# Low parts of projection weights by an adding DMA, and attention's first keys projected inside GLA

## The chip, the cores and the metric

One core of a Trainium2 chip runs the kernel. The metric is device time in microseconds (us), the median of several executions. The core has five engines that run side by side, each in the order of its own instructions: TensorE (PE: matmuls; PEld is its weight load), VectorE (DVE), ScalarE (ACT), GpSimd (POOL) and SyncE (SP, which issues DMAs here). DMAs that SP issues go through one queue; those that POOL issues go through another, whose descriptors are made in software.

## The reference, cut to what matters

One encoder layer over 1024 tokens of width 1024, all in float32:

```python
n = rmsnorm(h, ln_g)
proj = n @ w_in                      # 1024 x 3104
qa, ka, va, qg, kg, vg, rg, zf, zb = split(proj)
y_na  = neighbourhood_attention(qa, ka, va, rpb)   # 8 heads x 64, on a 16 x 64 grid
y_gla = bidirectional_gla(qg, kg, vg, rg, zf, zb)  # 4 heads, chunks of 64
h = h + concat([y_na, y_gla]) @ w_out
h = h + square(relu(rmsnorm(h) @ w1)) @ w2
out = rmsnorm(h)
```

## The kernel before, in words

Everything is held with the features on the 128 partitions and the tokens along them. A float32 product is made of three passes of a shorter format (fp32r): each operand is split into a high part, which is the value rounded, and a low part, which is the rest, and `product` issues high by high, high by low and low by high.

The input projection is cut into 24 blocks of 128 columns: 0, 1 are GLA's queries and 2, 3 its keys (two heads each), 4 to 7 its values `v`, 8 to 11 its output gate `r`, 12 to 15 attention's queries, 16 to 19 its keys and 20 to 23 its values (two heads each, a "pair"). A block's weights are 128 x 1024 values, 512 KB. Blocks 0 and 2 are loaded and split at the start by other code (`load_w`). All the others go through `proj`, which calls `weights`: SP loads the block into `wf` (L165); `split` has ACT round it into `wh` (L173) and POOL subtract to give `wl` (L174). Each of the tiles `wf`, `wh` and `wl` has two buffers. Then, for each half of the tokens, 24 matmuls (eight steps of three) fill a PSUM bank, and an evacuation `ev` multiplies by the row norm `rms` and writes what the block is for.

The stages follow one another: norm of the input with the first projections; GLA, head by head; attention, pair by pair; the output projection; the MLP, which is over half of the time. PE executes its matmuls in the order in which the program issues them. The other engines' order comes from a scheduler, with a few priorities given by hand (`SOON_W` for weights).

In GLA and in attention the projections' steps serve as filler: `Fill` holds a list of generators, and `fill.run(n)` issues `n` steps of three matmuls each. `FILL_ORDER` is the order of the blocks in GLA, and `GLA_FILL[h]` says how many steps go at each of eleven places of head `h`:

- 0: after `gla_keys` (decayed keys and queries on DVE and ACT); 1: after `gla_ktok` (keys transposed, L116); 2 and 3: after the two halves of `gla_contrib` (`c`; its copies into `st` are ACT's), the latter with `gla_scan` (28 steps on DVE, L566 and L569);
- 4 and 5: after the halves of `gla_within` (scores `a` within chunks, masked into `asb` by DVE, L561); after 5 the gates of the next head (`gla_gates`: `la` on PE, then ACT, then DVE's scans into `b`, L490 and L492);
- 6 and 7: after `gla_intra`; 8 and 9: after `gla_inter`; 10: after the first half's norm (`gla_norm`: `ov` on PE, then ACT and DVE; it ends with the write to `yg`, L595).

GLA's blocks and attention's first queries have 176 steps; the table and the two runs ahead of it ask for 192, so that the list is empty from place 6 of the last head on.

After GLA, attention's first keys are projected without anything between their matmuls (`run(na_proj(0, "k", ...))`), then eight steps (`NA_PRE`) of its first values, then the scores of pair 0, block 0 (`softmax`, L752). `bias_for` loads the bias tile `bt` (L693) and finishes it on DVE with the mask `msk` (L698). The key tiles are three of 128 x 1024 for each of two alternating pairs, `k00`, `k10`, `k20` and `k01`, `k11`, `k21`: the high part of the first head, that of the second, and the low part of both. `na_proj`'s `ev` writes a high part twice by ACT (L393, L395) and a low part by DVE (L397; for queries POOL does it).

Memory is a stack from either end. GLA's tiles are in pools on the right (`gla0`, `gla`), attention's on the left (`na` with `msk` and `bt`, `qkv` with the keys); both use the same addresses, one after the other. A tile that uses an address again waits for the last user of the memory before it.

Of the kernel before, what the change touches and what calls it, by code (L numbers as in the profile page):

```python
# [10 lines left out]
F32 = mybir.dt.float32  # L11
F32R = mybir.dt.float32r
U32 = mybir.dt.uint32
AF = mybir.ActivationFunctionType
ALU = mybir.AluOpType
# [3 lines left out]
P = 128  # L19
D = 1024  # L20
T = 1024
H = 512
# [15 lines left out]
GLA_MID = 7  # L38
GLA_LATE = 8
GLA_FILL = (  # L40
# [4 lines left out]
)  # L45
FILL_ORDER = (('v', 0), ('r', 0), ('v', 1), ('q', 1), ('r', 1), ('v', 2), ('v', 3), ('r', 3), ('r', 2), ('n', 0))
SOON = 200
SOON_W = 100
SOON_O = 100
# [14 lines left out]
def block_kernel(ctx, tc, xT, g_mix, w_in, w_z, rpb, na_mask, gu, gb, g_gla, sel_f, sel_b,  # L64
                 rst, w_out, g_ff, w1, w2, g_fin, out):
    nc = tc.nc
    V, S, DMA, G = nc.vector, nc.scalar, nc.sync, nc.gpsimd

    L = "left"
    R = "right"  # L70
    pool = lambda name, side, bufs=1: tc.tile_pool(name=name, bufs=bufs, side=side)
# [7 lines left out]
    stg = stg_stack.enter_context(pool("stg", L, 2))  # L79
# [40 lines left out]
    class Fill:  # L120
# [24 lines left out]
        def run(self, steps=1 << 30):  # L145
            while steps > 0 and self.gens:
                steps -= self.step()
# [12 lines left out]

    def weights(block, eng=None):

        with tc.high_priority(offset=SOON_W):
            wf = stg.tile([P, D], F32, tag="wf", name="wf")
            DMA.dma_start(wf, block)  # L165
            return split(wf, eng)

    def split(wf, eng=None, steps=1):
        wh = stg.tile([P, D], F32R, tag="wh", name="wh")
        wl = stg.tile([P, D], F32R, tag="wl", name="wl")  # L170
        for i in range(steps):
            c = slice(i * D // steps, (i + 1) * D // steps)
            S.copy(wh[:, c], wf[:, c])  # L173
            (eng or V).tensor_tensor(wl[:, c], wf[:, c], wh[:, c].bitcast(F32), op=ALU.subtract)  # L174
        return wh, wl
# [50 lines left out]

    def proj(blk, evac):

        w = weights(w_in[blk], G)
        for hf in range(2):  # L230
            d = bank("mm", f"proj{blk}_{hf}")
            yield from proj_part(d, w, hf * H, H)
            evac(hf, d)

    fill = Fill()
    gla_stack = ExitStack()
    g0 = gla_stack.enter_context(pool("gla0", R))
    zT = g0.tile([P, T], F32R, tag="zT", name="zT")
# [5 lines left out]
    def qk_evac(g, which):  # L244

        dic, sc, t = ((qd, 0.125, "q"), (kd, 1.0, "k"))[which]
        for i in range(2):
            dic[2 * g + i] = g0.tile([P, T], F32, tag=f"{t}d{i}", name=f"{t}d{2*g+i}")

        def ev(hf, d):  # L250
            c = slice(hf * H, (hf + 1) * H)
            for i in range(2):
                dst = dic[2 * g + i]
                a, b = (slice(0, 64), slice(64, 128))[::1 - 2 * i]
                V.scalar_tensor_tensor(dst[a, c], d[a, :], sc, rms[a, c], op0=ALU.mult, op1=ALU.mult)  # L255
                S.copy(dst[b, c], dst[a, c])
        return ev
# [123 lines left out]
    def na_proj(p, nm, parts, tmp):  # L381

        def ev(hf, d):
            t = tmp()
            with tc.high_priority(offset=SOON):
                V.tensor_tensor(t, d, rms[:, hf * H:(hf + 1) * H], op=ALU.mult)
            x = [perm(x, hf) for x in parts]
            for i in range(2):  # L390
                own, other = slice(i * 64, i * 64 + 64), slice(64 - i * 64, 128 - i * 64)
                ti, hi = nat(t[own, :]), x[i][own]
                S.copy(hi, ti)  # L393
                if nm == "k":
                    S.copy(x[i][other], ti)  # L395
                lo, eng = (x[2][own], V) if nm == "k" else (x[i][other], G)
                eng.tensor_tensor(lo, ti, hi.bitcast(F32), op=ALU.subtract)  # L397
        return proj({"q": 12, "k": 16}[nm] + p, ev)
# [3 lines left out]
    q0 = [yn_p.tile([P, T], F32R, tag=f"yn{2 + i}", name=f"q0{i}") for i in range(2)]  # L402
# [16 lines left out]
                          rpb1[:, :, :, 15 - r:31 - r, :].rearrange("c h d a b -> c (h d) (a b)"))  # L419

    with pool("gla", R) as gp:
        vtok, keep = {}, {}
        gated, normed = set(), set()
        masks = []

# [176 lines left out]
        def first_q(_):  # L602
            return na_proj(0, "q", q0, lambda: gp.tile([P, H], F32, tag="g1", name="qt", bufs=2))

        def go(n):
            fill.run(n)

        for kind, i in FILL_ORDER:
            gen = {"v": gla_v, "r": gla_r, "q": gla_qk, "n": first_q}[kind](i)
            fill.add(gen, (kind, i))  # L610
        go(GLA_PRE)
        bs = {0: gla_gates(0, GLA_MID)}
# [72 lines left out]
    with pool("na", L) as ap, pool("qkv", L) as qp:  # L685
# [16 lines left out]
        def qk_tiles(p):  # L702

            f = lambda pl, tag: pl.tile([P, T], F32R, tag=tag, name=f"{tag}p{p}")
            q = q0 if p == 0 else [f(yn_p, "yn3"), f(qp, "qc")] if p == 2 else [f(qp, "qa"), f(qp, "qb")]
            return q, [f(qp, f"k{i}{p % 2}") for i in range(3)]

        def na_v(p):

            vT = []  # L710

            def transposes():
                vhl[p] = ap.tile([P, NB, 2, P], F32R, tag="vhl", name=f"vhl{p}")
                for g in range(2):
                    tb = bank("mm" if p + 1 == NH // 2 else "t", f"nvt{p}_{g}")
                    for i in range(4):
                        j = 4 * g + i
                        PE.transpose(tb[:, i * P:(i + 1) * P], vT[0][:, j * P:(j + 1) * P], ident)
                    src = tb.rearrange("p (a h d) -> p a h d", a=4, h=2)
                    hi = vhl[p][:, 4 * g:4 * g + 4, :, 0:64]  # L720
                    with tc.high_priority(offset=SOON_V):
                        S.copy(hi, src)
                        V.tensor_tensor(vhl[p][:, 4 * g:4 * g + 4, :, 64:128], src, hi.bitcast(F32),
                                        op=ALU.subtract)

            def ev(hf, d):

                if not hf:
                    vT.append(qp.tile([P, T], F32, tag=f"k2{1 - p % 2}", name=f"vT{p}"))
                with tc.high_priority(offset=SOON):  # L730
                    V.tensor_tensor(perm(vT[0], hf), nat(d), nat(rms[:, hf * H:(hf + 1) * H]), op=ALU.mult)
                if hf:
                    fill.later(NA_LATE, transposes, ("v", p))
            return proj(20 + p, ev)
# [81 lines left out]

        qt = lambda: qp.tile([P, H], F32, tag="qt", name="qt", bufs=2)
        qk = qk_tiles(0)
        run(na_proj(0, "k", qk[1], qt))
        fill.add(na_v(0), ("v", 0))  # L820
        bt = bias_for(0)
        fill.run(NA_PRE)
# [1 line left out]
        for p in range(NH // 2):  # L824
            if p > 1:
                yn.append(yn_p.tile([P, T], F32, tag=f"yn{p}", name=f"yn{p}"))
            if p + 1 < NH // 2:
                nxt = qk_tiles(p + 1)
                fill.add(na_proj(p + 1, "q", nxt[0], qt))
                fill.add(na_proj(p + 1, "k", nxt[1], qt), ("k", p + 1))  # L830
                fill.add(na_v(p + 1), ("v", p + 1))
            pt = [[ap.tile([P, 3, 3, P], F32R, tag=f"pt{i}{j}", name=f"pt{p}{i}{j}") for j in range(2)]
                  for i in range(2)]
            ob = {}
            for b in range(NB):
                fill.at(NA_FILL, p, b, 0)
                if b + 1 < NB:
                    xn = softmax(p, b + 1, *qk, bt)
                fill.at(NA_FILL, p, b, 1)
                turn(p, b, xs, pt)  # L840
                if b + 1 == NB and p + 1 < NH // 2:
                    fill.until(("k", p + 1))
                    qk, bt = nxt, bias_for(p + 1)
                    fill.run(NA_NEXT)
                    xn = softmax(p + 1, 0, *qk, bt)
                xs = xn
                fill.at(NA_FILL, p, b, 2)
                if b == 2:
                    fill.until(("v", p))
                    pv(p, 0, pt, ob)  # L850
                if b > 1:
                    pv(p, b - 1, pt, ob)
                if b == 2 and p + 1 == NH // 2:

                    n_stack.close()
                    hT = ctx.enter_context(pool("h", R)).tile([P, NK, T], F32, tag="hT", name="hT")
                    a1 = ctx.enter_context(pool("a1", R))
                    yhl[0] = half(a1, "y0")
                    DMA.dma_start(hT[:, :, 0:H], xT[:, :, 0:H])
                    to_parts(0, KO[:2], V)  # L860
                    for d in range(NK):
                        fill.add(sums(0, d, KO[:-1], G, ahead=KO[2:-1] if d == 0 else ()))
            pv(p, NB - 1, pt, ob)
# [621 lines left out]
```

## Time and profile before

| | |
|---|---|
| median of 3 runs | 1203.62 us (1203.04 to 1208.0) |
| profiled execution | 1203.34 us, its span 1201.6 us, mean granted TensorE clock 0.991 |
| PE, DVE, ACT, POOL busy | 1156.0, 896.8, 646.3, 282.6 us |
| PE matmuls | 5632 |
| POOL's subtractions `wl` (L174) | 36 (22 for `proj`'s blocks, 14 for `w_out`) |
| ACT's casts `wh` (L173) | 43 |

Times in rows of the timeline are microseconds from the start of the span. A row there reads: start, length, engine, line, operation, output<-inputs, shapes, count, and in brackets how long the engine had been idle before it and what ended that. The granted clock is 1.00 when TensorE's throttle lets all of it through.

### The profile page before, as it was taken

The page shows a single profiled execution, that of the slowest core. Times are in us where ns is not written, and L with a number is a line of the kernel's source. Part 1 is how long each engine was busy: PE and PEld are TensorE (multiplying, and loading weights), DVE is VectorE, ACT ScalarE, POOL GpSimd, SP SyncE. Part 2 cuts the span into 40 slices and gives each one's busy share as a digit, 9 for nine tenths or more (in the row PEclk, how much of TensorE's full clock was granted, in tenths as well). Part 3 has the DMA queues.
Part 4 walks back from the last instruction along what each step waited for, and adds up shares of the span by engine and source line. Part 5 has one row for each costly group of instructions (what it writes and reads, how often), then busy time and mean ns, then how long its engine had stood idle before and what let it go on. Part 6 is the DMA issues. An engine that isn't in the chain of part 4 may idle for free.

```text
span 1201.6 us, 15423 instructions
## 1 busy us (share of the span) xinstructions
PE 1156.0 (96%) x5632; PEld 946.8 (79%) x5632; DVE 896.8 (75%) x1558; ACT 646.3 (54%) x1201; POOL 282.6 (24%) x199
## 2 busy tenths in 40 slices
PE   9998999899999999999999999999999999999995
PEld 8877777687877878877778888888888888888775
DVE  8787778767868785695858885877859768597467
ACT  6766565545555665444643635546355463454654
POOL 5311101122131323530103230412304114041003
PEclk9999999999999999999999999999999999999998
DMA  7111010110111142230210122111211122111203
GB/s 236 50 58 52 25 36 19 35 57 19 49 36 49 32 156 92 104 123 1 70 59 26 58 70 69 35 55 53 71 53 35 53 70 70 53 36 53 71 1 140
DMA packets 37259, 73.02 MB, mean 61 GB/s; under 512 B 8928, under 2 KB 20320, under 8 KB 37184
## 3 DMA queue, kind: packets, MB, share of 16 engines
q1 hardware_dynamic: 36608, 71.11, 17.7%
q8 instruction: 44, 0.72, 0.2%
q0 software_dynamic: 432, 0.93, 0.2%
q14 instruction: 31, 0.25, 0.1%
q10 hardware_dynamic: 144, 0.00, 0.0%
HBM read 67.84 MB, written 5.96 MB: 61 GB/s over the span
## 4 chain that ended last, share of the span: by engine, by line
PE 70%; DVE 18%; ACT 8%; issue 2%; DMA 1%; SPq 0%; POOL 0%; DVEq 0%; ACTq 0%
PE f L111 24%; PE u L111 21%; PE proj L111 12%; PE op L111 5%; PE sc L111 2%; PE no L111 2%; PE pt L116 1%; DVE st L569 1%; DVE nl L284 1%; DVE b L492 1%; DVE b L490 1%; DVE st L566 1%; DVE pl L958 1%; DVE nf L888 1%; DVE fsq L1388 1%
## 5 line engine op out<-in xcount | busy, mean ns | idle before, releaser
L958 POOL TENSOR_TENSOR ul<-uB,uh 128x512 fp32r<-128x512 f32 x84 | 109.2, 1319 | 330.4 <-ACT uh L993 213.4
L980 ACT CAST ph<-A 128x512 fp32r<-128x512 f32 x166 | 103.0, 621 | 146.2 <-PE f L111 73.6
L174 POOL TENSOR_TENSOR wl<-wf,wh 128x1024 fp32r<-128x1024 f32 x36 | 88.8, 2467 | 333.8 <-ACT wh L173 310.6
L111 PE MATMUL f<-uh,ph 128*128 128x512 f32 x400 | 155.8, 390 | 1.5 <-ACT u L1001 1.4
L111 PE MATMUL f<-ul,ph 128*128 128x512 f32 x400 | 155.7, 389 | 0.1
L111 PE MATMUL f<-uh,pl 128*128 128x512 f32 x400 | 155.7, 389 | 0.0
L958 DVE TENSOR_TENSOR pl<-A,ph 128x512 fp32r<-128x512 f32 x166 | 112.8, 689 | 52.6 <-ACT ph L980 52.6
L111 PE MATMUL proj<-nh,wh 128*128 128x512 f32 x352 | 150.9, 429 | 0.8 <-DVE qd L255 0.8
L111 PE MATMUL proj<-nh,wl 128*128 128x512 f32 x352 | 139.6, 397 | 0.0
L111 PE MATMUL proj<-nl,wh 128*128 128x512 f32 x352 | 139.4, 396 | 0.0
L1140 DVE TENSOR_TENSOR hT<-hT,f 128x512 f32<-128x512 f32 x168 | 113.0, 687 | 19.9 <-PE f L111 19.9
L111 PE MATMUL u<-n,ph 128*128 128x512 f32 x288 | 89.2, 391 | 2.0 <-ACT ph L893 2.0
L111 PEld LDWEIGHTS f<-uh,ph 128*128 128x128 f32 x400 | 75.1, 188 | 17.9 <-ACT u L1001 1.8
L111 PEld LDWEIGHTS f<-ul,ph 128*128 128x128 f32 x400 | 75.1, 188 | 16.0 <-DVE ul L958 0.4
L111 PEld LDWEIGHTS f<-uh,pl 128*128 128x128 f32 x400 | 75.1, 188 | 15.6
L111 PEld LDWEIGHTS proj<-nh,wh 128*128 128x128 f32 x352 | 66.9, 190 | 19.8 <-issue 5.2
L993 ACT CAST uh<-uB 128x512 fp32r<-128x512 f32 x84 | 51.9, 618 | 51.3 <-PE f L111 34.5
L111 PE MATMUL u<-T,ph 128*128 128x512 f32 x256 | 79.2, 391 | 0.1
L111 PEld LDWEIGHTS proj<-nh,wl 128*128 128x128 f32 x352 | 67.1, 191 | 15.2
L111 PEld LDWEIGHTS proj<-nl,wh 128*128 128x128 f32 x352 | 67.4, 191 | 11.5 <-issue 1.4
L111 PE MATMUL op<-y,wh 128*128 128x512 f32 x240 | 75.8, 396 | 0.4 <-DVE y L665 0.4
L111 PE MATMUL u<-nt,ph 128*128 128x512 f32 x224 | 68.9, 389 | 0.0
(297 smaller groups left out, 2484.5 us busy)
## 6 DMA issues: line engine op xcount, KB each, us to landing
A<-in_w SPq DMA_DIRECT2D x64, 512.0 KB
wf<-in_w_in SPq DMA_DIRECT2D x22, 512.0 KB
wf<-in_w_out SPq DMA_DIRECT2D x17, 512.0 KB
hT<-in_xT SPq DMA_DIRECT2D x2, 2048.0 KB
xs<-in_xT SPq DMA_DIRECT2D x6, 512.0 KB
out<-hT SPq DMA_DIRECT2D x4, 512.0 KB
out<-hT SPq DMA_DIRECT2D x8, 256.0 KB
rpb<-rpb SPq DMA_DIRECT2D x16, 96.0 KB
```

The lines of the kernel that those rows point to most:

```text
L111: m = nc.tensor.matmul(*args, **kw)
L116: tc.keep_in_program_order(nc.tensor.transpose(*args, **kw))
L174: (eng or V).tensor_tensor(wl[:, c], wf[:, c], wh[:, c].bitcast(F32), op=ALU.subtract)
L284: V.scalar_tensor_tensor(nl[:, k, sl], xs[:, k, :], gmix[:, k:k + 1], nh[:, k, sl].bitcast(F32), op0=ALU.mult, op1=ALU.subtract)
L490: V.tensor_tensor_scan(b[0:64, c], rsts[0:64, :], m[0:64, :], 0.0, op0=ALU.mult, op1=ALU.add)
L492: V.tensor_tensor_scan(b[64:128, c][:, ::-1], rsts[64:128, ::-1], m[64:128, ::-1], 0.0, op0=ALU.mult, op1=ALU.add)
L566: V.scalar_tensor_tensor(st[0:64, i + 1, :], st[0:64, i, :], dec[0:64, i:i + 1], st[0:64, i + 1, :], op0=ALU.mult, op1=ALU.add)
L569: V.scalar_tensor_tensor(st[64:128, j - 1, :], st[64:128, j, :], dec[64:128, j:j + 1], st[64:128, j - 1, :], op0=ALU.mult, op1=ALU.add)
L958: return kp(eng.tensor_tensor(l, x, h.bitcast(F32), op=ALU.subtract))
L980: kp(S.copy(ph, x))
L993: kp(S.copy(uh, x))
L1140: kp(V.tensor_tensor(hT[:, d, c], hT[:, d, c], o[:, s], op=ALU.add))
```

## The change

`weights` has a second way to make a block's low part, used for all of `proj`'s blocks but block 4: ACT writes the negated rounded weights into `wl`, and a DMA issued by POOL adds the block, read again from HBM, to it; ACT then makes `wh` with a pass of its own. The output projection's weights keep `split`.

Attention's first keys become the last entry of `FILL_ORDER`, `("k", 0)`, and their projection ahead of attention is gone. The table asks for eight more steps: two at place 5 of head 0, one at place 5 of head 2, one at place 1 and four at place 3 of head 3. Counted through, that puts four of the 16 steps ahead of the last head's second `gla_contrib` (they push later blocks' steps forward) and twelve at its places 3 to 8. So that the tiles exist then, GLA's first and second query and key tiles and the key tiles `k00`, `k10`, `k20` share a new pool `glak`, which lies on the right under GLA's others and is closed late in attention.

```diff
-    (17, 4, 3, 3, 5, 3, 2, 3, 6, 0, 3),
+    (17, 4, 3, 3, 5, 5, 2, 3, 6, 0, 3),
     (8, 2, 5, 2, 4, 2, 3, 3, 5, 0, 4),
-    (10, 4, 3, 4, 4, 3, 4, 3, 6, 0, 2),
-    (13, 3, 3, 4, 3, 2, 3, 3, 3, 0, 7),
+    (10, 4, 3, 4, 4, 4, 4, 3, 6, 0, 2),
+    (13, 4, 3, 8, 3, 2, 3, 3, 3, 0, 7),
...
-FILL_ORDER = (..., ('r', 2), ('n', 0))
+FILL_ORDER = (..., ('r', 2), ('n', 0), ('k', 0))
...
             DMA.dma_start(wf, block)
-            return split(wf, eng)
+            if eng is not None:
+                return split(wf, eng)
+            wl = stg.tile([P, D], F32R, tag="wl", name="wl")
+            S.activation(wl, wf, AF.Copy, scale=-1.0)
+            G.dma_start(wl, block, accum_op=ALU.add)
+            wh = stg.tile([P, D], F32R, tag="wh", name="wh")
+            S.copy(wh, wf)
+            return wh, wl
...
-        w = weights(w_in[blk], G)
+        w = weights(w_in[blk], G if blk == 4 else None)
...
+    k_stack = ExitStack()
+    gk = k_stack.enter_context(pool("glak", R))
...
-            dic[2 * g + i] = g0.tile([P, T], F32, tag=f"{t}d{i}", name=f"{t}d{2*g+i}")
+            dic[2 * g + i] = (g0 if t == "q" and i else gk).tile([P, T], F32, tag={"k0": "k00", "q0": "k10", "k1": "k20"}.get(f"{t}{i}", "qd1"), name=f"{t}d{2*g+i}")
...
+        def first_k(_):
+
+            k0.extend(gk.tile([P, T], F32R, tag=f"k{i}0", name=f"k{i}0p0") for i in range(3))
+            yield from na_proj(0, "k", k0, lambda: gp.tile([P, H], F32, tag="g1", name="qt", bufs=2))
...
-            return q, [f(qp, f"k{i}{p % 2}") for i in range(3)]
+            return q, k0 if p == 0 else [f(qp if p % 2 else gk, f"k{i}{p % 2}") for i in range(3)]
...
-                    vT.append(qp.tile([P, T], F32, tag=f"k2{1 - p % 2}", name=f"vT{p}"))
+                    vT.append((gk if p % 2 else qp).tile([P, T], F32, tag=f"k2{1 - p % 2}", name=f"vT{p}"))
...
-        run(na_proj(0, "k", qk[1], qt))
...
+                    k_stack.close()
                     n_stack.close()
```

More of the change, by code (lines that the diff above doesn't have):

```diff
@@ L40 @@
 GLA_FILL = (
[1 row of a table removed]
[1 row of a table added]
     (8, 2, 5, 2, 4, 2, 3, 3, 5, 0, 4),
[2 rows of a table removed]
[2 rows of a table added]
 )
-FILL_ORDER = (('v', 0), ('r', 0), ('v', 1), ('q', 1), ('r', 1), ('v', 2), ('v', 3), ('r', 3), ('r', 2), ('n', 0))
+FILL_ORDER = (('v', 0), ('r', 0), ('v', 1), ('q', 1), ('r', 1), ('v', 2), ('v', 3), ('r', 3), ('r', 2), ('n', 0), ('k', 0))
 SOON = 200
@@ L421, in block_kernel @@
     with pool("gla", R) as gp:
-        vtok, keep = {}, {}
+        vtok, k0 = {}, []
         gated, normed = set(), set()
@@ L608, in block_kernel @@
         for kind, i in FILL_ORDER:
-            gen = {"v": gla_v, "r": gla_r, "q": gla_qk, "n": first_q}[kind](i)
+            gen = {"v": gla_v, "r": gla_r, "q": gla_qk, "n": first_q, "k": first_k}[kind](i)
             fill.add(gen, (kind, i))
```

## The prediction

> **What bounds the kernel now.** I read the busy shares first, then the busy time by stage, then the slow instructions of DVE beside POOL, then TensorE's waits. The page's head and its engine rows, with the row of the removed instruction:
>
> ```profile
> span 1201.6 us, 15423 instructions
> PE 1156.0 (96%) x5632; PEld 946.8 (79%) x5632; DVE 896.8 (75%) x1558; ACT 646.3 (54%) x1201; POOL 282.6 (24%) x199
> L174 POOL TENSOR_TENSOR wl<-wf,wh 128x1024 fp32r<-128x1024 f32 x36 | 88.8, 2467 | 333.8 <-ACT wh L173 310.6
> ```
>
> TensorE (PE) is busy for 96% and does the same matmuls after the change, so at most its idle time and its slow-clock time can be won. Busy time by stage says where these lie (columns: engine busy times with counts, then the granted clock, the DMA engines' share, GB/s):
>
> ```profile
> 60.00:252.00 192.00, 174.73 (x999) 139.44 (x998) 150.26 (x239) 109.40 (x176) 32.00 (x20) 0.96 0.12 38
> 252.00:440.00 188.00, 185.34 (x945) 147.98 (x944) 146.18 (x392) 113.27 (x276) 42.11 (x24) 1.00 0.12 40
> 120.00:140.00 20.00, 17.56 (x108) 13.32 (x107) 15.62 (x35) 8.61 (x14) 2.38 (x1) 0.91 0.13 37
> 180.00:200.00 20.00, 17.96 (x106) 14.80 (x102) 15.67 (x26) 7.31 (x12) 2.36 (x1) 0.91 0.07 27
> 235.00:246.00 11.00, 7.86 (x35) 6.08 (x34) 9.60 (x21) 0.62 (x1) 1.04 (x1) 0.69 0.00 0
> ```
>
> GLA (60 to 252) leaves PE idle for 192.0 - 174.7 = 17.3 us and loses clock after its waits: (1 - 0.91) x 20 = 1.8 us twice and (1 - 0.69) x 11 = 3.4 us near its end. Attention (252 to 440) leaves 2.7 us. All that this change can win is about 27 us.
>
> What makes PE wait in GLA is the DVE chain, and POOL's subtraction lengthens it. The timeline, POOL's row first, then DVE's:
>
> ```profile
> 56.32 2.76 POOL L174 TENSOR_TENSOR wl<-wf,wh 128x1024 fp32r<-128x1024 f32 x1 [2.91 <-ACT wh L173]
> 55.67 1.22 DVE L490 TENSOR_TENSOR_SCAN b<-rsts,lm 64x512 f32<-64x512 f32 x1
> 56.90 3.26 DVE L492 TENSOR_TENSOR_SCAN b<-rsts,lm 64x512 f32<-64x512 f32 x1
> 87.19 1.57 DVE L569 SCALAR_TENSOR_TENSOR st<-st,dec 64x128 f32<-64x128 f32 x1
> 89.51 2.67 DVE L569 SCALAR_TENSOR_TENSOR st<-st,dec 64x128 f32<-64x128 f32 x7
> 126.26 3.80 DVE L566 SCALAR_TENSOR_TENSOR st<-st,dec 64x128 f32<-64x128 f32 x7
> 147.59 3.43 DVE L490 TENSOR_TENSOR_SCAN b<-rsts,lm 64x512 f32<-64x512 f32 x1
> 183.45 2.21 DVE L569 SCALAR_TENSOR_TENSOR st<-st,dec 64x128 f32<-64x128 f32 x1
> ```
>
> The reader is to see one scan take 1.22 and the next 3.26 us, with POOL's subtraction beside it; a step of the state scan takes 2.67 / 7 = 0.38 us, but 1.57 or 2.21 when it is caught. The PE rows with a wait, and what ended it:
>
> ```profile
> 71.02 1.09 PE L116 MATMUL kt<-ident,kD 128*128 128x128 f32 x8 [1.43 <-DVE kD L508]
> 93.00 0.50 PE L111 MATMUL la<-zT,guh 128*128 128x512 f32 x1 [2.36 <-DVE asb L561]
> 134.29 0.48 PE L111 MATMUL a<-qD,kI 64*128 64x128 f32 x2 [0.94 <-DVE asb L561]
> 167.58 1.13 PE L116 MATMUL kt<-ident,kD 128*128 128x128 f32 x8 [0.70 <-ACT nu L205]
> 186.47 1.16 PE L111 MATMUL a<-qD,kI 64*128 64x128 f32 x14 [2.04 <-DVE asb L561]
> 239.66 0.80 PE L111 MATMUL a<-qD,kI 64*128 64x128 f32 x2 [2.80 <-DVE asb L561]
> 240.79 2.07 PE L111 MATMUL a<-qD,kI 64*128 64x128 f32 x14 [0.34 <-DVE asb L561]
> ```
>
> That the stalled instructions lie on the way to the end is shown by the chain that ended last, in which they stand (start, length, piece):
>
> ```profile
> 56.90 3.27 DVE b L492
> 87.19 1.57 DVE st L569
> ```
>
> **Part 1: low parts by an adding DMA.** 21 of the 22 weight blocks that `proj` loads (all but block 4) lose the POOL subtraction: 21 x 2.467 = 51.8 us less on POOL. Each gains a second 128x1024 pass on ACT and a DMA that POOL issues.
>
> Stalls won, each the smaller of DVE's excess and the PE wait behind it: 3.26 - 1.22 = 2.0 against 1.43, take 1.4; 1.57 - 0.38 = 1.2 at 93.00, of which the two fill steps added there leave 1.0; 3.80 - 2.67 = 1.1 against 0.94, take 0.9; 3.43 - 1.22 = 2.2 against 0.70, take 0.7; 2.21 - 0.38 = 1.8 against 2.04, take 1.8. Sum -5.8 us; ends 0 (another wait ends last) and -7.5 (the five waits whole). Two clock drops follow these waits (those of 120 to 140 and 180 to 200). I take both as gone, -3.6 us; ends 0 and -3.6.
>
> ACT's added passes, by rows of ACT and of PE:
>
> ```profile
> 221.06 1.03 ACT L173 CAST wh<-wf 128x1024 fp32r<-128x1024 f32 x1
> 224.19 1.16 PE L111 MATMUL c<-vtok,kt 64*128 64x128 f32 x16 [1.08 <-ACT kt L525]
> ```
>
> Some ten of the 21 fall in GLA. Where ACT then idles or DVE is the later one, 1.05 us more costs nothing. Here at 221.06 ACT already makes PE wait. I count two of ten on the path, +2.1 us; ends 0 and 10 x 1.05 = +10.5. ACT in attention is busy for 113 of 188 us and gets 11 x 1.05 = 11.6 more, while DVE loses its stalls. PE's projection steps cover both, and I take 0; ends -2.7 (the stage's whole idle time) and +3 (three passes caught).
>
> The adding DMA must land before the third matmul of a step of its block. Rows of the first and the last of the 21 blocks (`r` of head 0, `v` of attention's last pair): the cast, the first matmul with `wl`; and what DMAs from POOL's queue took for 256 KB (last column: issue to landing):
>
> ```profile
> 46.28 1.04 ACT L173 CAST wh<-wf 128x1024 fp32r<-128x1024 f32 x1
> 56.01 0.39 PE L111 MATMUL proj<-nh,wl 128*128 128x512 f32 x1
> 399.67 1.05 ACT L173 CAST wh<-wf 128x1024 fp32r<-128x1024 f32 x1
> 417.32 0.40 PE L111 MATMUL proj<-nh,wl 128*128 128x512 f32 x1
> rsts<-in_rst POOLq DMA_DIRECT2D x1, 256.0 KB, 8.5
> msk<-in_na_mask POOLq DMA_DIRECT2D x1, 256.0 KB, 3.4
> ```
>
> From the end of the pass to the use stand 56.0 - 47.3 = 8.7 us and 417.3 - 400.7 = 16.6 us; worked out alike, the others have 11.7, 12.5, 13.4, 14.2 and then 15.9 or more. No row has an adding DMA of 512 KB. Its bounds are 3.4 us (undisturbed, if bytes cost little) and 17 us (twice the queued 8.5). It is nearest to the undisturbed row, since the queue is otherwise empty: some 6 us, all hidden, 0; ends 0 and +29 us (17 us against each block's time). The second reading of 0.5 MB x 21 over 380 us adds 29 GB/s to 38, where the DMA engines are busy for 0.12: free. POOL waits for ACT as before; behind it stand `st`'s memsets and the low parts of the queries, which then come earlier. `wf` is freed by ACT, not POOL, so SP's loads are issued about 2.4 us sooner.
>
> The Trainium skill, "DMA: Bandwidth & Descriptors", section "Anatomy of one DMA", fits such a DMA as 2.0 us plus its bytes over 436 GB/s; with the two source reads that "Collectives: The Full Stack" counts for an add (section "The bandwidth ceiling"), an estimate is 4.4 us, and the term stays 0.
>
> **Part 2: first attention keys inside GLA.** Sixteen fill steps (48 matmuls) leave the place between GLA and attention: four go ahead of head 3's second contribution, twelve into its tail. Of the four, two lie in the wait at 93.00 (counted), one in that at 224.19, and one costs +0.7 us on the way. The rows of the seam (the first is the chain's, 24 steps without a break, 0.68 us each):
>
> ```profile
> 252.90 16.33 PE proj L111 x72
> 260.60 0.68 DVE L397 TENSOR_TENSOR k20p<-qt,k00p 64x512 fp32r<-64x512 f32 x1
> 262.63 0.69 DVE L595 TENSOR_TENSOR yg<-ny,o 128x512 f32<-128x512 f32 x1
> 263.52 0.38 SPq L693 DMA_DIRECT2D bt<-rpb  x1
> 265.21 2.48 DVE L397 TENSOR_TENSOR k20p<-qt,k00p 64x512 fp32r<-64x512 f32 x1 [0.69 <-ACT k00p L393]
> 269.11 1.82 DVE L698 SCALAR_TENSOR_TENSOR bt<-bt,msk 128x384 f32<-128x384 f32 x4
> 271.45 0.42 DVE L752 CUSTOM_DVE_ANT_0 xsc<-sc,bt 128x256 f32<-128x256 f32 x1
> ```
>
> Twelve steps in the tail are 8.2 us. They fill its wait (2.80 + 0.34 us) and its clock loss (3.4), 6.5 in all, so the norm starts 1.6 us later. But attention cannot start when PE is free: the bias `bt` is loaded into GLA's memory, right behind its last norm (`yg`, ended 263.3), and the first softmax waits for it. The change leaves this as it is. The norm and the bias are rid of key work on DVE: two halves of 0.7 us inside the norm, one between the bias's parts. So the first softmax moves by +1.6 - 1.4 - 0.7 = -0.5 us, though 10.9 us of PE work have left its way. PE, with eight steps of `v`, its scores and four steps more, is done some 8 us early and waits for `bt`: a new wait, which eats the filled one. Ends: +1.6 (DVE's relief doesn't reach) and -2.3 (the stalled 2.48, 1.8 over its neighbours' 0.68, counts whole as well). A wait of that length brings a clock drop; by the two 1.8 us rows, +1.8; ends 0 and +3.4.
>
> The keys' own evacuation (eight casts of ACT, six of DVE's 0.7 us) lies beside the tail's steps. Their `wf` load passes on SP ahead of `bt`, as before, and their adding DMA on POOL ahead of the mask's.
>
> **Sum.** -5.8 - 3.6 + 2.1 + 0 + 0 + 0.7 - 0.5 + 1.8 = -5.3 us. The profiled execution took 1203.3 us (span 1201.6), about the median of 1203.62. Forecast 1198.0 us.
>
> **The rivals.**
> Late adding DMAs (slower). For it: nothing here shows one, and POOL makes its descriptors while DVE is 78% busy (150.26 of 192). Against: the spare times. At 17 us each the blocks are late by 29 us together, 1227; it decides (slower by over 0.5%) from about 14.4 us on, where 11 us are lost. The Trainium skill, "SBUF — State Buffer", section "SBUF: two separate sides", has this rule: POOL is locked out of writing descriptors while DVE runs an instruction that takes both ports. If that held for all of DVE's busy time, 3.4 us would become 3.4 / 0.22 = 15.5 us and 17 us would be lost.
> ACT takes DVE's place: all ten passes on the path, 8.4 us over my two, 1206. For: 224.19. Against: ACT is busy for only 109 of 192 us.
> The stalls were not the limit, and the clock drops stay: +9.4, 1207. Against: the stalled rows in the chain.
> More is won: no ACT cost, no drop at the seam, attention's 2.7 us gone: 1191.4.
>
> **How the numbers follow.** About 0.5%, 6 us, is what can be told from no change; the border is 1197.6. Forecast case 0.50 (1194 to 1202): 0.31 faster, 0.19 same. More won 0.14, faster. ACT or no limit 0.23: 0.19 same, 0.04 slower. Late DMAs 0.13: 0.11 slower, 0.02 same. Faster 0.45, same 0.40, slower 0.15. The range, 1191 to 1206, leaves out the late DMAs and the ends of the others.
>
> **What would show it.** The scans all at 1.22 us and the state steps at 0.38; PE waits under 1 us at 71, 134 and 186 with the clock at 1.00 there; none at the second `a` of head 3; a wait of some 8 us ahead of the scores of block 1, ended by `bt`; `proj` with `wl` never waiting for a DMA. I am wrong if PE waits for `wl`, if ACT ends the waits that DVE ended, or if the seam's wait is far from 8 us.

## The result, and the profile after

The changed kernel takes 1218.8 us (median; 1218.1 to 1219.3) against 1203.5 us: 1.0118 of the time before, with an interval of 1.0094 to 1.0143. It is slower by some 15 us, where 1198 was forecast and 1191 to 1206 was the range.

The page of the changed kernel, as the lines shown of before, with the added DMA's issues:

```profile
span 1216.1 us, 15445 instructions
PE 1164.6 (96%) x5632; PEld 953.5 (78%) x5632; DVE 874.8 (72%) x1558; ACT 665.2 (55%) x1222; POOL 246.4 (20%) x199
wl<-in_w_in POOLq DMA_DIRECT2D x21, 512.0 KB, 7.8
```

DVE is busy for 22 us less, POOL for 36 less, ACT for 19 more. The adding DMA lands after 7.8 us (its last column; the forecast assumed 6, and the estimate of 4.4 beside it falls further short), and no wait of PE in this trace was ended by it. PE is busy for 8.6 us more with the same 5632 matmuls, which fits the stretches at half clock below. The waits of PE that are new or grew, or were forecast to go and stayed:

```profile
106.92 0.77 PE L111 MATMUL proj<-nh,wh 128*128 128x512 f32 x1 [4.99 <-DVE qd L265]
247.04 0.49 PE L111 MATMUL a<-qD,kI 64*128 64x128 f32 x2 [2.80 <-DVE asb L571]
266.38 1.90 PE L111 MATMUL ov<-osq,ones 128*128 128x512 f32 x2 [2.13 <-ACT osq L595]
284.59 0.69 PE L111 MATMUL sc<-k00p,q 128*128 128x384 f32 x1 [6.45 <-DVE sm L767]
```

The reader is to see that none of them names `wl`. The granted clock (the figure after POOL's, 0.5 where it is halved) drops behind the first three of them and, at the fourth, from within the wait; busy times in those windows:

```profile
106.40:116.60 10.20, 9.68 (x29) 7.72 (x30) 0.98 (x2) 3.57 (x7) 0.40 (x2) 0.51 0.63 153
249.80:253.20 3.40, 3.40 (x15) 2.94 (x13) 1.52 (x3) 0.39 (x1) 0.00 (x0) 0.54 0.00 0
266.80:270.20 3.40, 3.40 (x8) 2.02 (x7) 1.24 (x2) 2.55 (x5) 0.00 (x0) 0.53 0.73 143
280.50:290.70 10.20, 5.98 (x16) 4.21 (x17) 6.89 (x24) 3.26 (x10) 0.00 (x0) 0.51 0.12 45
```

The same PE instructions set side by side with before say where the time went. At head 0's first state products (`o<-qD,st`, at 100 us before) the changed kernel leads by 2.9 us; at head 0's first norm matmul (113) it is 5.2 late. At head 3's second contribution (233) it is 4.8 late, at its first norm matmul (263) 12.3, at the scores of block 2 (292) 15.0. From there to the end of the kernel it stays between 13 and 15. Two places lose all of it: 107 us, and the stretch from 233 us on, that is GLA's tail and the seam between GLA and attention.

Place one. DVE's rows and what the wait of 4.99 us was for (`qD` of head 1 reads `qd`, then the next heads' `qd` is written into the same memory):

```profile
104.84 1.21 DVE L524 TENSOR_TENSOR qD<-qD,qd 128x1024 f32<-128x1024 f32 x1
106.08 1.30 DVE L265 SCALAR_TENSOR_TENSOR qd<-proj,rms 64x512 f32<-64x512 f32 x2
```

`proj` has two PSUM banks. The 17th step of blocks 1 and 3 opens a third and needs the first back, whose evacuation writes `qd` where head 1's queries still lie. Before, that step stood at place 10 of head 0. The two steps added at place 5 move it to place 8, ahead of head 0's last state products, and PE, in order, stands in front of it.

Place two, from the last norm to the first softmax, on DVE, SP and POOL:

```profile
274.68 0.69 DVE L746 TENSOR_TENSOR vT<-proj,rms 128x512 f32<-128x512 f32 x1 [2.89 <-PE proj L111]
277.46 0.69 DVE L605 TENSOR_TENSOR yg<-ny,o 128x512 f32<-128x512 f32 x1
278.35 0.38 SPq L708 DMA_DIRECT2D bt<-rpb  x1
278.75 0.56 POOL L702 DMA_DIRECT2D msk<-in_na_mask  x1 [14.15 <-DVE yg L605]
282.30 1.90 DVE L713 SCALAR_TENSOR_TENSOR bt<-bt,msk 128x256 f32<-128x256 f32 x5 [4.15 <-DMA msk<-in_na_mask]
284.11 0.41 DVE L767 CUSTOM_DVE_ANT_0 xsc<-sc,bt 128x256 f32<-128x256 f32 x1
```

The last norm ends at 278.15, 14.8 us later than before; the bias load goes out 0.2 us behind it, the mask's 0.6 us. DVE's row names the mask as the one that landed last; both lie in memory that GLA used, and both wait for this norm.

### The profile page after: what moved, and what is told of

Its sections match the earlier page's. It is cut to its first block, busy times and chain, and to the rows that moved or that the text cites. A ratio compares the mean times of both kernels' runs of the same rounds, so it can differ in the third digit from the quotient of the medians.

```text
span 1216.1 us, 15445 instructions
## 1 busy us (share of the span) xinstructions
PE 1164.6 (96%) x5632; PEld 953.5 (78%) x5632; DVE 874.8 (72%) x1558; ACT 665.2 (55%) x1222; POOL 246.4 (20%) x199
## 4 chain that ended last, share of the span: by engine, by line
PE 76%; DVE 13%; ACT 6%; issue 2%; DMA 1%; SPq 0%; POOL 0%; DVEq 0%; ACTq 0%; POOLq 0%
PE f L111 24%; PE u L111 21%; PE proj L111 15%; PE op L111 5%; PE sc L111 2%; PE no L111 2%; DVE st L579 1%; PE pt L116 1%; PE o L111 1%; DVE pl L973 1%; DVE asb L571 1%; DVE nf L903 1%; PE sb L111 1%; PE ob L111 1%; DVE st L576 1%
## 5 line engine op out<-in xcount | busy, mean ns | idle before, releaser
L111 PE MATMUL proj<-nh,wh 128*128 128x512 f32 x352 | 153.8, 437 | 6.8 <-DVE qd L265 5.0
L111 PEld LDWEIGHTS proj<-nh,wh 128*128 128x128 f32 x352 | 68.2, 194 | 26.5 <-issue 5.9
L171 POOL DMA_DIRECT2D wl<-in_w_in x21 | 18.7, 891 | 266.7 <-ACT wl L170 248.6
```

What stands on the lines that cost most here:

```text
L111: m = nc.tensor.matmul(*args, **kw)
L171: G.dma_start(wl, block, accum_op=ALU.add)
```

## The experiments

Theory A: the adding DMA wins what was forecast, and the moved projection steps lose more. Theory B: the loss comes with the adding DMA (ACT's passes, late low parts). Behind each median stands its ratio to the kernel before, measured in the same group of runs, with a 95% interval; the kernel before had 1205.4, 1203.9, 1203.9 and 1205.2 us in the four groups, and 1203.5 in that of the result. A difference between medians of two groups, such as one to the changed kernel's 1218.8, is therefore good to about 2 us only.

**One part at a time.** The adding DMA alone:

```diff
 kernel before
+            if eng is not None: return split(wf, eng)
+            ... adding DMA as in the change
-        w = weights(w_in[blk], G)
+        w = weights(w_in[blk], G if blk == 4 else None)
```

> The kernel before with the adding DMA alone (21 blocks), attention's first keys where they were. Theory A (the loss is the moved projection steps: at 107 us PE stands 5 us in front of a full bank, and at the seam it waits for the bias): this is faster than before by 4 to 9 us, 1194 to 1200, with no wait over 2 us at 107 and none at the scores of block 1. Theory B (the loss comes with the adding DMA, by the added ACT passes or by low parts that land late): 1208 to 1218, with both waits in place.

Measured: 1195.3 us, 0.9915 (0.990 to 0.993). 10 us faster, theory A's range; B falls. At the second contribution of head 3 it leads by 8.9 us, and at the end of the two traces by 8.4.

The keys alone:

```diff
 changed kernel
-        w = weights(w_in[blk], G if blk == 4 else None)
+        w = weights(w_in[blk], G)
```

> The changed kernel with all low parts subtracted by POOL again; the keys inside GLA and the changed table stay. Theory A: 1213 to 1222, about as slow as the changed kernel or slower, with the wait at the scores of block 1 over 5 us. Theory B: 1200 to 1206.

Measured: 1231.9 us, 1.0215 (1.020 to 1.023): slower than even A allowed. Both waits are there (4.99 and 6.45 us), PE stands for another 5.38 us behind the gate's evacuation (`rm`), and the wait in front of head 3's second scores has doubled:

```profile
230.93 0.79 PE L111 MATMUL proj<-nh,wh 128*128 128x512 f32 x1 [5.38 <-DVE rm L460]
...
260.13 0.79 PE L111 MATMUL a<-qD,kI 64*128 64x128 f32 x2 [5.91 <-DVE asb L571]
```

So the parts are -10 and +26.5 us alone, +15 together.

**The first place.** Two steps moved from place 5 to place 10:

```diff
-    (17, 4, 3, 3, 5, 5, 2, 3, 6, 0, 3),
+    (17, 4, 3, 3, 5, 3, 2, 3, 6, 0, 5),
```

> The changed kernel with the two added steps of head 0 moved from place 5 to place 10, behind the last state products and the first norm. Theory A: the wait of 5 us at 107 and the clock drop of 10.2 us behind it go, 8 us are won there, some of it lost again later: 1209 to 1214. Theory B: 1217 to 1220, since the bank is late for another reason than the steps' place.

Measured: 1211.4 us, 1.0053 (1.0036 to 1.0070). The wait at that bank is back to what it was, and 7.4 us of the changed kernel's median are won (in the traces 8.0 us at head 3's second contribution, 6.1 at the last matmul):

```profile
107.59 0.47 PE L111 MATMUL proj<-nh,wh 128*128 128x512 f32 x1 [0.82 <-DVE qd L265]
```

The same entry put into the good kernel:

```diff
 adding DMA alone
-    (17, 4, 3, 3, 5, 3, 2, 3, 6, 0, 3),
+    (17, 4, 3, 3, 5, 5, 2, 3, 6, 0, 3),
```

> The adding DMA alone, with the one table entry of the change, two more steps at place 5 of head 0. Theory: these bring the third bank of the next projections ahead of head 0's last state products; PE stands 5 us at 107 and the clock drops behind it: 1200 to 1206. Rival (the wait needs the other entries too): 1194 to 1197.

Measured: 1209.3 us, 1.0037 (1.0021 to 1.0052). The one number costs 14 us here, more than expected: 7.6 us at the bank, and later another clock drop of 20.5 us (from 238 us on), where every later place has other steps; that these are the reason was not tested apart.

```profile
106.81 0.76 PE L111 MATMUL proj<-nh,wh 128*128 128x512 f32 x1 [4.99 <-DVE qd L262]
```

**The second place.** Pair 0's bias replaced (it is left out, and old values stand in its stead, so nothing is waited for):

```diff
-        bt = bias_for(0)
+        bt = nl.rearrange("p k t -> p (k t)")[:, 0:14 * P].bitcast(F32)...
```

> The changed kernel; pair 0 of attention takes as its bias a part of a tile that has long been there (low parts of the normed input) in place of the loaded and masked bias, so its softmax doesn't wait for GLA's memory. Theory A: the wait of 6.45 us ahead of the scores of block 1 goes, and the clock drop of 10.2 us behind it: 1206 to 1211. Rival: the seam is late because ACT and DVE are, whatever the bias waits for: 1215 to 1219.

Measured: 1209.4 us, 1.0031 (1.0020 to 1.0043), 9.4 us under the changed kernel. Not all of this is the bias: the trace leads by 2.5 us at the scores of block 0 already, since at the same wait of 4.99 us at 107 the clock is halved for 3.4 us here and for 10.2 in the changed kernel's trace. From there to the scores of block 2 the lead grows to 10.5 us, so the seam wins 8.0. The wait of 6.45 us is down to:

```profile
276.24 0.44 PE L111 MATMUL sc<-k00p,q 128*128 128x384 f32 x1 [0.65 <-DVE sm L767]
```

Its control, the same edit where nobody waited for the bias:

> Control: the adding DMA alone (1195.3), and pair 0 takes the same long present tile in place of its bias. There PE did not wait at the seam, so taking the bias away should win nothing: 1193 to 1196. If it is faster than 1191, leaving the bias out wins by itself, and its gain in the other kernels is to be read with that taken off.

Measured: 1195.1 us, 0.9921 (0.9906 to 0.9936), the same as with the bias (1195.3): leaving it out wins nothing by itself.

Both edits, place 10 and no bias:

> The changed kernel with both edits that won something: two steps moved to place 10 of head 0, and a long present tile in place of pair 0's bias. If the two losses are independent: 1218.8 - 7.4 - 9.4 = 1202, still some 7 us over the adding DMA alone, with no wait over 3 us. If one is only passed on: 1206 or more.

Measured: 1202.7 us, 0.9991 (0.9978 to 1.0004). The two losses add up, as far as medians of three groups can tell (1202 expected). The 7.4 us left over the adding DMA alone lie ahead of the norm: head 3's second contribution is 4.6 us later than there and its first norm matmul 12.4; the 16 key steps that no longer stand behind it give some of that back.

More work for PE ahead of the scores, in the place-10 kernel:

```diff
-NA_PRE = 8
+NA_PRE = 16
```

> The changed kernel with the two steps at place 10 of head 0, and with 16 in place of 8 steps of attention's first values ahead of its first scores, so that PE has work where it waits for the bias. If the seam's loss is PE standing without cover (6.5 us and the clock drop behind it): 1203 to 1207 against 1211. If the bias chain sets the time whatever PE does: 1210 to 1213.

Measured: 1216.1 us, 1.0101 (1.008 to 1.012), against 1211.4. At the seam it does what it should: the scores of block 3 come 3.4 us earlier, 1.0 of which the trace led by ahead of the seam. But the steps are then missing in attention, and near its end PE waits again and runs at half clock for 13.7 us:

```profile
275.00:441.00 166.00, 156.78 (x801) 123.80 (x799) 119.52 (x350) 102.00 (x250) 26.01 (x21) 1.00 0.27 64
441.00:455.00 14.00, 11.12 (x38) 8.48 (x39) 12.66 (x35) 9.72 (x26) 2.55 (x2) 0.51 0.79 291
```

**Where the keys may stand.** The table of before, with the keys in the list:

> The changed kernel with the table of before: no step of other blocks is moved, nine key steps lie at places 6 to 8 of head 3 and seven between its two norms. If every place ahead of the last norm costs, since the bias waits for that norm: 1199 to 1206, with a wait of 3 to 7 us ahead of the scores of block 1. If only the added entries of the table cost: 1193 to 1197.

Measured: 1204.3 us, 0.9997 (0.998 to 1.001). All of the adding DMA's gain is gone, though by less PE waiting than expected (1.6 us at the scores of block 1): the norm ends 7.3 us later than with the adding DMA alone (262.1 against 254.8). The bias load goes out later still, at 263.6, 0.2 us behind the keys' last low part, which DVE does after that norm. Nine key steps stand behind the wait at head 3's second scores here, and it stays 2.78 us.

The same, with the keys behind the last norm's matmuls, where they stood:

```diff
-    (13, 4, 3, 8, 3, 2, 3, 3, 3, 0, 7),
+    (13, 3, 3, 4, 3, 2, 0, 0, 0, 0, 0),
```

> The changed kernel with the table of before, and nothing at places 6 to 10 of head 3: the keys are in the fill list and in the new pool, but their 16 steps come after the last norm's matmuls, where they stood before. If only the steps' place costs: as fast as the adding DMA alone, 1193 to 1198. If the new pool, the shared buffers or the keys' tiles cost something: 1200 or more.

Measured: 1205.5 us, 1.0012 (0.9998 to 1.0025). That missed 1193 to 1198: the place of the steps alone is not the reason. The bias still comes late, and SP's own waits say for whom. First the adding DMA alone, then this kernel (us waited in total, times, longest; then DVE's and SP's rows of this kernel):

```profile
SPq L700 <- DVE yg L602: 15.9, 1, 15.9
```

```profile
SPq L708 <- DVE k20p L407: 2.1, 1, 2.1
...
262.47 0.69 DVE L407 TENSOR_TENSOR k20p<-qt,k10p 64x512 fp32r<-64x512 f32 x1 [0.60 <-ACT k10p L403]
...
263.36 0.38 SPq L708 DMA_DIRECT2D bt<-rpb  x1
```

Before, the keys' temporary `qt` lay in attention's memory; now it lies in GLA's pool, whose addresses `bt` takes, so the bias waits for the end of the keys' evacuation (263.2) and not of the norm (255 in the adding DMA alone). Once out, the load also took longer:

```profile
270.80 1.90 DVE L713 SCALAR_TENSOR_TENSOR bt<-bt,msk 128x256 f32<-128x256 f32 x5 [5.81 <-DMA bt<-rpb]
```

DVE has the bias 7.4 us after its issue; in the changed kernel bias and mask were both there 4.0 us after it. A weight block's load and adding DMA had gone out 2.7 and 2.4 us ahead of the bias, and from 263.4 to 267.0 us the DMA engines were busy for 0.97; I take that for the reason, but no run tells the two delays apart. An attempt to detach the bias from the keys, with `qt` in a tile of GLA's other pool:

> As the kernel with the keys last (1205.5), but the keys' temporary lies in a tile of the other, earlier GLA pool, so that the pool whose memory the bias takes ends with the norm again. If that kernel was slow because the bias waited for the keys' evacuation: back to the adding DMA alone, 1194 to 1198, with the bias loaded right after the last norm. If the key tiles' new pool costs: 1202 to 1206.

Measured: 1203.5 us, 0.9993 (0.9977 to 1.0009), 2 us less, with intervals that overlap. The load still went out right behind the keys' last low part (260.1, load at 260.3): the temporary holds it from this tile as well, so the edit didn't test what it should. The bias taken away instead:

> The keys in the fill list and after the last norm's matmuls (1205.5), and pair 0 takes a long present tile in place of its bias. If all of that kernel's loss over the adding DMA alone is the bias that waits for the keys' evacuation in GLA's memory: 1193 to 1197, with no wait ahead of the scores of block 1. If the key tiles' pool or the shared temporary cost by themselves: 1200 or more.

Measured: 1199.8 us, 0.9958 (0.9944 to 0.9973). 6 of the 10 us were the bias's wait; 1199.8 lies between the two forecasts. Against the adding DMA with the same tile in place of its bias (1195.1, in the same group) 4.7 us are left. Two waits show there that I read as their cause, and neither is for the key tiles: a bank that waits because `qt` shares two buffers with the norm's temporaries, and DVE waiting for the mask, which also lies behind the keys:

```profile
250.91 0.50 PE L111 MATMUL proj<-nh,wh 128*128 128x512 f32 x1 [2.23 <-DVE qt L398]
...
266.93 0.43 DVE L713 SCALAR_TENSOR_TENSOR bt<-bt,msk 128x256 f32<-128x256 f32 x1 [3.34 <-DMA msk<-in_na_mask]
```

**What the adding DMA wins.** POOL's old subtraction put back beside it:

```diff
 adding DMA alone
             S.copy(wh, wf)
+            G.tensor_tensor(wf, wf, wh.bitcast(F32), op=ALU.subtract)
```

> The adding DMA alone (1195.3), and POOL also does its old subtraction of 128x1024 for each of the 21 blocks, into wf, where nobody reads it; only the load of a later block waits for it. If the gain came from POOL's instruction no longer stopping DVE: the gain goes, 1202 to 1207. If it came from wl being ready at another time or from the order of ACT: 1194 to 1198.

Measured: 1227.0 us, 1.0178 (1.0145 to 1.0212). The gain goes, as expected, and 20 us more with it, which wasn't. Groups of DVE, each of one shape (count, busy us, mean ns), the adding DMA alone first, then with the subtraction:

```profile
L764 DVE TENSOR_SCALAR xsc<-xsc,sm 128x384 f32<-128x384 f32 x48 | 21.2, 441 | 1.4
L576 DVE SCALAR_TENSOR_TENSOR st<-st,dec 64x128 f32<-64x128 f32 x56 | 20.6, 368 | 1.9
```

```profile
L765 DVE TENSOR_SCALAR xsc<-xsc,sm 128x384 f32<-128x384 f32 x48 | 32.6, 679 | 1.4
L577 DVE SCALAR_TENSOR_TENSOR st<-st,dec 64x128 f32<-64x128 f32 x56 | 26.3, 469 | 1.9
```

The same DVE instructions take 679 and 469 ns with POOL's subtraction, 441 and 368 without. This bears out the direction, that POOL's subtraction slows DVE; the size it doesn't, since the loss is 32 us where 10 had been won. Why stays open; the added ACT pass and the later loads of `wf` are in this kernel too.

**A faster version.** The adding DMA alone is it. One attempt to better it, by two steps moved ahead of head 3's second scores:

```diff
-    (13, 3, 3, 4, 3, 2, 3, 3, 3, 0, 7),
+    (13, 3, 3, 4, 5, 0, 3, 3, 3, 0, 7),
```

> The adding DMA alone with head 3's two steps of place 5 moved to place 4, ahead of the second scores, where PE waits 2.8 us for DVE and its clock then drops for 6.8 us. If PE then stands for less than 2 us and the clock holds: 1190 to 1194. If DVE's scan, which sets the end of that stage, is only met by PE later: 1194 to 1196.

Measured: 1199.0 us, 0.9940 (0.992 to 0.996), 3.7 us worse than without (3.5 in the traces) and outside both forecasts. The wait goes from those scores to the products behind them, and the clock drop becomes longer (10.2 us in place of 6.8):

```profile
236.87 1.73 PE L111 MATMUL o<-asb,vtok 128*128 128x128 f32 x8 [2.78 <-DVE asb L568]
```

## Why the prediction was wrong

Part 1 was right, and in its mechanism. Its stalls, clock and ACT terms were -5.8 - 3.6 + 2.1 = -7.3 us; the adding DMA alone led by 8.9 at the end of that stretch (8.4 at the end of the traces, 10 in the medians). Its five waits of PE were 7.5 us long before; at the same matmuls 1.6 are left, so 5.9 went where 5.8 were forecast. All 16 of DVE's scans take 1.22 us there, where the longest took 3.43. The clock drops of 120 to 140 and 180 to 200 did not occur in its trace. Only ACT's +2.1 does not show as a wait: the wait at 224.19 shrank from 1.08 to 0.25 us instead of growing. The DMA stayed hidden: 7.8 us against a shortest spare time of 8.7. The rule of the locked port, which made a rival (the Trainium skill, "SBUF — State Buffer", section "SBUF: two separate sides"), shows in a row only the other way round (DVE stopped by POOL's arithmetic); the DMAs landed within 6.4 to 8.5 us beside a busy DVE, so starved descriptors made no late block here.

The sum failed in part 2, at the three steps that follow, in the prediction's words; the last term of the sum held.

"Of the four, two lie in the wait at 93.00 (counted)". I priced those steps by the wait they fill and forgot that a list of fill moves every later step forward. A step that opens a third bank came ahead of head 0's last state products: +8.1 us between the first state products and the norm, where the sum has +0.7 for the four steps; +7.4 at the end (the place-10 kernel).

"They fill its wait (2.80 + 0.34 us) and its clock loss (3.4), 6.5 in all, so the norm starts 1.6 us later." From head 3's second contribution to its first norm matmul the changed kernel lost 12.3 - 4.8 = 7.5 us, nearly the whole 8.2 of the twelve steps: they filled next to nothing. The wait stands at the second scores, behind places 3 and 4. Eight of the twelve steps, those at places 6 to 8, come after it and could not fill it. The four at place 3 come ahead of the first scores, and DVE's masks went back with them. DVE's rows, the kernel before first (its first mask, after 20 of the 28 steps of the state scan), then the changed kernel (after 26):

```profile
238.88 0.72 DVE L561 COPY_PREDICATED asb<-selF,a 128x512 f32<-128x512 uint32 x1
```

```profile
241.65 4.58 DVE L579 SCALAR_TENSOR_TENSOR st<-st,dec 64x128 f32<-64x128 f32 x7
246.26 0.72 DVE L571 COPY_PREDICATED asb<-selF,a 128x512 f32<-128x512 uint32 x1
```

From the contribution to that mask are 10.7 us before and 13.3 now: 2.6 more, about what the four steps take, so the wait stayed 2.80. Every kernel here with eight steps at place 3 of head 3 has 26 scan steps ahead of the mask, every other one 20. That the order follows from these steps is read from the traces; no run moves them alone. The 4.58 us (2.67 for seven undisturbed steps) come from the first queries' low parts, which POOL does beside them (2.63 us from 241.90 on); before, two steps of the same scan took 1.29 and 1.32 us for the same reason, so this is no new loss. Of the clock loss, half was won: 3.4 us at half clock in place of 6.8.

"So the first softmax moves by +1.6 - 1.4 - 0.7 = -0.5 us". Against the second contribution of head 3 it moved by 12.7 - 4.8 = +7.9: the 7.5 us above, and +0.4 where DVE's relief was to give -2.1. "The keys' own evacuation lies beside the tail's steps" was wrong for ACT: a weight block's two passes and four key casts stood ahead of the second square, and PE waited 2.13 us for it.

```profile
262.37 1.05 ACT L170 ACTIVATE wl<-wf 128x1024 fp32r<-128x1024 f32 x1
...
265.22 0.62 ACT L405 CAST k10p<-qt 64x512 fp32r<-64x512 f32 x1
...
265.75 0.59 ACT L595 ACTIVATE osq<-o 128x512 f32<-128x512 f32 x1
```

And the second norm's DVE work stood behind the first values' evacuation, which waited 2.89 us for PE: moving the keys away had moved those values into the norm.

"A wait of that length brings a clock drop; by the two 1.8 us rows, +1.8". The wait was foreseen (8 us forecast, 6.45 measured, ended by the bias), and the clock term was near: the clock was halved for 10.2 us, of which 4.3 lie in the wait itself, and of the 8.0 us that the seam wins without the bias 5.8 are the wait, so 2.2 are left for the clock. What failed stood ahead of it: the wait was to cost nothing beyond this, since PE would be early and the norm hardly move; the norm moved by 7.5 us.

The rival on the slow side was the wrong one: late DMAs. The mechanism that held attention back, the bias behind GLA's last user, was in the prediction; what it missed is how late that user becomes when the filler in front of it fills no wait.

## What to carry to other kernels

Filler moved towards a wait is not free because PE is idle there: with in-order issue, follow every later step that it shifts to the bank, buffer and evacuation that step needs, and price each engine's queue at the new place. Steps behind the wait can't fill it, and steps ahead of it may put off the very work that it waits for. Look for what the next stage really waits for, here loads that wait for the last user of the memory below it: cover taken away from in front of such loads comes back as a wait, here with a clock drop on top. And measure the parts of a change alone; here one part won 0.8% and the other hid it.

## What the runs showed of the hardware that was not expected

The halved clock can outlast the wait that it follows by far, and by different lengths: in or behind the same wait of 4.99 us at the same bank, in the traces of four kernels, the clock was halved for 3.4, 6.8, 6.8 and 10.2 us (the shortest and the longest in two kernels that differ only in attention's first bias), and in one kernel a stretch of 20.5 us went with waits of 2.7 and 1.7 us among short matmuls. All stretches at half clock that are named here are multiples of some 3.4 us. An adding DMA of 512 KB from POOL's queue took 6.4 to 8.5 us from issue to landing in the changed kernel, and its issue held POOL for 0.85 to 1.04 us, against 2.4 us for the subtraction.
